# An expert stage on one core: adding products and transposes moved into the branches of the weight products

## The chip, the cores and the metric

The kernel runs on one core of a Trainium2 chip. The metric is the device time of one execution in microseconds (us), the median of several runs. The engines are TensorE (PE, matmuls; PEld is its weight load, PEq its sequencer), VectorE (DVE), ScalarE (ACT), GpSimd (POOL) and SyncE (SP, which issues the loads).

## The reference, cut to what matters

The program is two layers of a hybrid block on 256 tokens of 1024 channels, all in float32. The second layer ends in a mixture of eight experts; each token goes to the two experts with the highest router logits. This is the stage of the change:

```python
D_FF_EXPERT = 3584; N_EXPERTS = 8; TOP_K = 2
def swiglu(x, wg, wu, wd):
    return (jax.nn.silu(x @ wg) * (x @ wu)) @ wd
def moe_swiglu(x, router, wg, wu, wd):
    ...
    for e in range(N_EXPERTS):
        y = y + gate[:, e:e + 1] * swiglu(t, wg[e], wu[e], wd[e]).astype(jnp.float32)
```

## The kernel before, in words

**Tokens.** For each expert the kernel gathers that expert's tokens (at most 128, else a slow way at the end) into a tile `xg`, transposed, as two float32r parts that add up to the float32 value (a high and a low part). The same is done with every weight: a piece of 1 MB is loaded by SP into a tile `w` (or `big`), ACT rounds half a piece to its high part (line 347, 128x1024), and DVE subtracts to get the low part (line 348, 128x1024). Such a pair of halves is one tile `wp`; four of them rotate.

**Units.** The 3584 hidden columns of an expert are worked in seven slices of 512. A unit is one expert and one slice, 56 units in all. The loop in `moe` does for each unit, in this order: the gate half (`half_mm`, four weight products), the up half (`half_mm`, four), and then the down products of the unit before (`down`, four). One weight product (`products`) uses one pair of halves. So there are twelve pairs to a unit, and each needs one cast on ACT, one subtraction on DVE and one product on PE. The orders of PE, ACT and DVE in this stage are as the code writes them.

**Two branches.** PE reads how many tokens the expert has (`many[e]`). With more than 64 (`HALF`), a product is six matmuls (lines 376 to 378: high x high, high x low, low x high for two slices of the channels). With at most 64, the tokens' high and low part lie side by side in one stationary operand, and a product is four matmuls (line 1562). The rows 64 to 127 of the result then hold the low tokens' share, and it must be added to rows 0 to 63: ACT copies it to a tile `low` (line 1580, `lower`), and PE adds it with a matmul with a shifted identity, the adding product (`folded`, line 1586). In the branch of many tokens there is nothing to add; there `folded` multiplies zeros (line 1589), 64x8. `folded` has a branch of its own (line 1585).

**Transposes.** h = silu(gate) x up of a unit (`hidden`, line 1593, and `hidden_times`, line 1596; tile `sgm`) is transposed on PE in the next unit, between its gate and its up half (`turn`), with four 128x128 transposes (line 1603) or eight of 64 rows (line 1608), again in a branch of its own (line 1601). ACT and DVE then split the result into the two parts of `hT` (`split_from_psum`, lines 386 and 387), which the down products read.

The experts are worked in pairs; gathering the next pair's tokens, the way back (`scatter`) and the like are small tasks that stand between the halves (`little`).

Of the kernel before, what the change touches and what calls it, by code (L numbers as in the profile page):

```python
# [19 lines left out]
P = 128  # L20
S = 256
D = 1024
KT = D // P
# [43 lines left out]
HALF = CAP // 2  # L67
# [204 lines left out]
def tile_hybrid_block(  # L272
    ctx: ExitStack, tc: tile.TileContext,
    x, x_t, w_in, mla_w_uq, mla_w_ukv, small, vecs, w_out, ln1_w, ln1_b, ffn_wg, ffn_wu, ffn_wd,
    router, moe_wg, moe_wu, moe_wd, ln2_w, ln2_b, cst, out, stop=None, dbg=None,
):
    nc = tc.nc
    pe, act, dve, pool, sp = nc.tensor, nc.scalar, nc.vector, nc.gpsimd, nc.sync
# [4 lines left out]
    def gap(pl, n, tag):  # L283

        pl.tile([P, n // 4], F32, tag=tag, bufs=1, name=tag)
# [13 lines left out]
    def bank(name="pm"):  # L299
        return psm.tile([P, 512], F32, tag="bank", name=name)  # L300
# [5 lines left out]
    def kept(name):  # L306
        o, n = _OFF[name]
        return ck[:, o:o + n]

    ident = kept("ident")  # L310
# [63 lines left out]
    def mm3(ps, s, m, first, last):  # L374

        pe.matmul(ps, s[0], m[0], start=first, stop=False)  # L376
        pe.matmul(ps, s[0], m[1], start=False, stop=False)  # L377
        pe.matmul(ps, s[1], m[0], start=False, stop=last)  # L378
# [6 lines left out]
    def split_from_psum(hi, lo, ps):  # L385
        act.copy(hi, ps)  # L386
        dve.tensor_tensor(lo, ps, hi.bitcast(F32), op=OP.subtract)
# [1024 lines left out]
    def moe(mp, free_order):  # L1412
        nonlocal x_sb

        fold = mp.tile([P, HALF], F32R, tag="fold", name="fold")
# [16 lines left out]
        many = {}  # L1432
# [42 lines left out]
        def soon_one():  # L1475
            if waiting:
                waiting.pop(0)()

        def soon_all():
            while waiting:  # L1480
                waiting.pop(0)()
# [50 lines left out]
        hs = {}  # L1532
# [8 lines left out]
                except StopIteration:  # L1541
                    tasks.pop(0)

        def products(e, todo):

            def plain():
                for ps, st, m, first, last in todo:  # L1550
                    mm3(ps, (st[:, 0], st[:, 1]), m, first, last)

            if e not in many:
                plain()
                return
            with tc.If(many[e] > HALF) as cmp:
                plain()
            with cmp.Else():
                for part in range(2):
                    for ps, st, m, first, last in todo:  # L1560
                        both = st.rearrange("p a s -> p (a s)")[:, HALF:HALF + P]
                        pe.matmul(ps, both, m[part], start=first and part == 0,  # L1562
                                  stop=last and part == 1)

        def half_mm(e, after={}):
            xg = state[e][0]
            ps = bank()
            for k in range(0, KT, 2):
                if k % 4 == 0:
                    pcs = feed.next()  # L1570
                m = pcs[k % 4 // 2]
                products(e, [(ps, xg[:, k + i], [q[:, i] for q in m], k + i == 0, k + i == KT - 1) for i in range(2)])
                soon_one()
                after.get(k // 2, lambda: None)()
            return ps, [] if e in many else None

        def lower(ps, low):
            if low is not None:
                low.append(mp.tile([P, 512], F32R, tag="sgm", bufs=SGM, name="low"))
                act.copy(low[0][HALF:], ps[HALF:])  # L1580

        def folded(e, ps, low):
            if low is not None:
                low, = low
                with tc.If(many[e] <= HALF) as cmp:
                    pe.matmul(ps[:HALF], fold[HALF:], low[HALF:], start=False, stop=True, skip_group_check=True)
                with cmp.Else():

                    pe.matmul(ps[:HALF, :8], fold[:HALF], fold[:HALF, :8], start=False, stop=True, skip_group_check=True)

        def hidden(e, s, pg):
            hs[e, s] = mp.tile([P, 512], F32, tag="sgm", bufs=SGM, name="sgm")
            act.activation(hs[e, s], pg, AF.Silu)

        def hidden_times(e, s, pu):
            dve.tensor_tensor(hs[e, s], hs[e, s], pu, op=OP.mult)

        def turn(e, s):
            last = (e, s) == UNITS[-1]
            pt = bank()  # L1600
            with tc.If(many[e] > HALF) as cmp:
                for j in range(4):
                    pe.transpose(pt[:, j * P:(j + 1) * P], hs[e, s][:, j * P:(j + 1) * P], ident)
            with cmp.Else():
                for j in range(4):
                    for i in range(2):
                        c = j * P + i * HALF
                        pe.transpose(pt[:, c:c + HALF], hs[e, s][:HALF, j * P:(j + 1) * P], ident[:HALF, :HALF])
            if last:
                hT = mp.tile([P, 4, 2, P], F32R, tag=XG[5], name="hl")  # L1610
            else:
                if not gapped:
                    gap(mp, GAPS[1], "gap1")
                hT = mp.tile([P, 4, 2, P], F32R, tag="hT", bufs=HTB, name="hT")
                if not gapped:
                    gapped.append(gap(mp, GAPS[2], "gap2"))
            hs[e, s] = hT
            return lambda: split_from_psum(hT[:, :, 0], hT[:, :, 1], pt.rearrange("p (j s) -> p j s", j=4))

        def down(e, s, after={}):  # L1620
            if s == 0:
                z[e] = [bank("z") for _ in range(2)]
            hT = hs.pop((e, s))
            for j in range(2):
                pw = feed.next()
                last = (e, s, j) == (*UNITS[-1], 1)
                for i in range(2):
                    products(e, [(z[e][h], hT[:, 2 * j + k],
                                  [q[:, k] for q in pw[h]] if last else [q[:, 0, h * 512:(h + 1) * 512] for q in pw[k]],
                                  s == 0 and j == k == 0, s == NS - 1 and j == k == 1)  # L1630
                                 for k, h in ([(0, i), (1, i)] if last else [(i, 0), (i, 1)])])
                    soon_one()
                    after.get(2 * j + i, lambda: None)()

# [44 lines left out]
        first = gather(ORDER[0])  # L1679
# [5 lines left out]
        prev = None  # L1685
# [4 lines left out]
        for i_, (e, s) in [(i // (2 * NS), u) for i, u in enumerate(UNITS)]:  # L1690
            if s == 0:
                soon_all()
            end = (e, s) == UNITS[-1]
            pg, low_g = half_mm(e)
            little()
            split_hidden = turn(*prev) if prev else lambda: None
            pu, low_u = half_mm(e, {0: split_hidden, 1: lambda: lower(pg, low_g), 3: lambda: folded(e, pg, low_g)})
            little()
            if prev:
                def product():  # L1700
                    folded(e, pu, low_u)
                    hidden(e, s, pg)
                    if end:
                        hidden_times(e, s, pu)

                down(*prev, {0: lambda: lower(pu, low_u), 1 if end else 2: product,
                             3: (lambda: turn(e, s)()) if end else lambda: hidden_times(e, s, pu)})
                if prev[1] == NS - 1:
                    tasks.append(scatter(prev[0]))
                    if prev[0] == ORDER[i_ - 1][1]:  # L1710
                        tasks.append(way_back(ORDER[i_]))
                    little()
            else:
                lower(pu, low_u)
                folded(e, pu, low_u)
                hidden(e, s, pg)
                hidden_times(e, s, pu)
            if (e, s) == (0, 2):

                x_sb = xpool.tile([P, 2, D], F32, tag="x", name="x_sb")  # L1720
                for t in range(2):
                    pool.tensor_tensor(x_sb[:, t], xh[:, t].bitcast(F32), xl[:, t].bitcast(F32), op=OP.add)
                    pool.tensor_scalar(x_sb[:, t], x_sb[:, t], ALPHA, None, op0=OP.mult)
            if s == 3 and e == ORDER[i_][0] and i_ + 1 < len(ORDER):
                tasks.append(gather(ORDER[i_ + 1]))
            if s > 1:
                little()
            prev = (e, s)
# [16 lines left out]
        with tc.If(v > CAP):  # L1745
            for e in range(NE):
# [3 lines left out]
                xg = mp.tile([P, KT, P], F32, tag="xg0", name="xg2")  # L1750
                for k in range(KT):
                    ps = bank()
# [10 lines left out]
                with tc.For_i(0, D_FE, P) as f0:  # L1763
# [8 lines left out]
                    ps = bank()  # L1772
# [3 lines left out]
                    hT = mp.tile([P, 512], F32, tag="sgm", bufs=SGM, name="hT2")[:, :P]  # L1776
# [6 lines left out]
                pt = bank()  # L1783
# [8 lines left out]
                for h in range(2):  # L1792
                    dve.tensor_scalar(z2[h], z2[h], gsl, None, op0=OP.mult)
                    for t in range(2):
                        ps = bank()
# [10 lines left out]
        for t in range(2):  # L1806
# [6 lines left out]
            for h in range(2):  # L1813
                c = slice(h * 512, (h + 1) * 512)
# [79 lines left out]
```

## Time and profile before

| what | value |
|---|---|
| median of 3 runs | 1429.23 us (1426.94 to 1429.64) |
| profiled execution | 1427.92 us |
| its span | 1426.2 us |
| PE busy | 1378.8 us (97%) |
| DVE busy | 1240.4 us (87%) |
| ACT busy | 1048.9 us (74%) |
| read from HBM | 428.19 MB |

The span runs from the first to the last instruction of the profiled execution; the rest of its time lies around it. Busy times are of the whole program: the first layer and the mixer of the second come before the experts, whose first Silu starts at 473.8 us. Matmuls are pipelined, so a matmul's duration (0.39 us for 128x512) is longer than the step from one start to the next (0.23 us), and it is the steps that add up to time.

### The profile page before, as it was taken

The page shows a single profiled execution, that of the slowest core. Times are in us where ns is not written, and L with a number is a line of the kernel's source. Part 1 is how long each engine was busy: PE and PEld are TensorE (multiplying, and loading weights), DVE is VectorE, ACT ScalarE, POOL GpSimd, SP SyncE. Part 2 cuts the span into 40 slices and gives each one's busy share as a digit, 9 for nine tenths or more (in the row PEclk, how much of TensorE's full clock was granted, in tenths as well). Part 3 has the DMA queues.
Part 4 walks back from the last instruction along what each step waited for, and adds up shares of the span by engine and source line. Part 5 has one row for each costly group of instructions (what it writes and reads, how often), then busy time and mean ns, then how long its engine had stood idle before and what let it go on. Part 6 is the DMA issues. An engine that isn't in the chain of part 4 may idle for free. (4 is left out here: it accounts for less than half of the span.)

```text
span 1426.2 us, 20823 instructions
## 1 busy us (share of the span) xinstructions
PE 1378.8 (97%) x7068; PEld 1091.3 (77%) x7068; DVE 1240.4 (87%) x1702; ACT 1048.9 (74%) x1384; POOL 57.3 (4%) x70
## 2 busy tenths in 40 slices
PE   9999999999999989999999999999999999999995
PEld 8888999987888756666788766678887876667774
DVE  7998645468788999999988899998889899999896
ACT  7743534436633879899888889988888888998884
POOL 1020000001011040000000000000000000000000
PEclk9999999999999999999999999999999999999998
DMA  9364736562258979999999999999999999999950
GB/s 342 123 230 130 256 133 220 177 231 90 105 212 327 384 256 393 391 386 402 402 375 345 340 371 397 402 402 357 337 335 353 361 362 378 391 402 401 371 188 35
DMA packets 200045, 431.19 MB, mean 302 GB/s; under 512 B 9824, under 2 KB 44000, under 8 KB 199904
## 3 DMA queue, kind: packets, MB, share of 16 engines
q1 hardware_dynamic: 195952, 425.01, 81.4%
q0 software_dynamic: 864, 3.15, 0.6%
q8 instruction: 93, 1.52, 0.4%
q10 hardware_dynamic: 3088, 1.11, 0.4%
q14 instruction: 48, 0.39, 0.1%
HBM read 428.19 MB, written 1.05 MB: 301 GB/s over the span
## 5 line engine op out<-in xcount | busy, mean ns | idle before, releaser
L348 DVE TENSOR_TENSOR wp<-w,wp 128x1024 fp32r<-128x1024 f32 (+2 forms) x676 | 789.7, 1205 | 112.1 <-ACT wp L347 100.9
L347 ACT CAST wp<-w 128x1024 fp32r<-128x1024 f32 (+2 forms) x676 | 679.2, 1030 | 170.7 <-PE pm L383 38.2
L1562 PE MATMUL pm<-wp,xg 128*128 128x512 f32 x848 | 225.8, 411 | 19.0 <-DVE wp L348 17.7
L1562 PEld LDWEIGHTS pm<-wp,xg 128*128 128x128 f32 x848 | 153.6, 192 | 76.8 <-DVE wp L348 46.2
L377 PE MATMUL pm<-wp,xg 128*128 128x512 f32 x472 | 184.5, 391 | 2.9 <-DVE wp L348 2.9
L376 PE MATMUL pm<-wp,xg 128*128 128x512 f32 x472 | 186.8, 396 | 0.0
L378 PE MATMUL pm<-wp,xg 128*128 128x512 f32 x472 | 184.1, 390 | 0.0
L1562 PE MATMUL z<-wp,hT 128*128 128x512 f32 x448 | 129.3, 418 | 0.7 <-DVE wp L348 0.7
L348 DVE TENSOR_TENSOR wp<-big,wp 128x1024 fp32r<-128x1024 f32 x100 | 119.0, 1221 | 6.8 <-ACT wp L347 5.3
L347 ACT CAST wp<-big 128x1024 fp32r<-128x1024 f32 x100 | 102.3, 1051 | 11.7 <-PE pm L378 8.2
L1562 PEld LDWEIGHTS z<-wp,hT 128*128 128x128 f32 x448 | 75.6, 188 | 41.6 <-DVE wp L348 21.3
L377 PEld LDWEIGHTS pm<-wp,xg 128*128 128x128 f32 x472 | 88.7, 188 | 22.2 <-DVE wp L348 4.9
L378 PEld LDWEIGHTS pm<-wp,xg 128*128 128x128 f32 x472 | 88.6, 188 | 18.7
L376 PEld LDWEIGHTS pm<-wp,xg 128*128 128x128 f32 x472 | 88.7, 188 | 17.8
L381 PE MATMUL pm<-big,wp 128*128 128x256 f32 x320 | 90.6, 283 | 0.0
L383 PE MATMUL pm<-big,wp 128*128 128x256 f32 x320 | 90.6, 283 | 0.0
L382 PE MATMUL pm<-big,wp 128*128 128x256 f32 x320 | 90.5, 283 | 0.0
L376 PE MATMUL z<-wp,hT 128*128 128x512 f32 x216 | 89.1, 413 | 0.0
L377 PE MATMUL z<-wp,hT 128*128 128x512 f32 x216 | 84.9, 393 | 0.4 <-DVE wp L348 0.4
L378 PE MATMUL z<-wp,hT 128*128 128x512 f32 x216 | 84.0, 389 | 0.0
L520 PE MATMUL pm<-wp,big 128*128 128x512 f32 (+1 forms) x288 | 69.7, 389 | 0.6 <-ACT big L386 0.2
L1580 ACT CAST low<-pm 64x512 fp32r<-64x512 f32 x109 | 63.5, 583 | 2.6
(323 smaller groups left out, 1859.9 us busy)
## 6 DMA issues: line engine op xcount, KB each, us to landing
w<-in_moe_w_gate_dram SPq DMA_DIRECT2D x93, 1024.0 KB, 7.9
w<-in_moe_w_up_dram SPq DMA_DIRECT2D x93, 1024.0 KB, 7.7
w<-in_moe_w_down_dram SPq DMA_DIRECT2D x92, 1024.0 KB, 7.3
big<-in_moe_w_gate_dram SPq DMA_DIRECT2D x17, 1024.0 KB, 6.6
big<-in_moe_w_up_dram SPq DMA_DIRECT2D x17, 1024.0 KB, 6.7
w<-in_w_in_dram SPq DMA_DIRECT2D x16, 1024.0 KB, 8.5
big<-in_moe_w_down_dram SPq DMA_DIRECT2D x16, 1024.0 KB, 8.9
w<-in_ffn_w_gate_dram SPq DMA_DIRECT2D x11, 1024.0 KB, 5.6
```

Of the source, the lines that this page charges most:

```text
L347: act.copy(hv[c], src_[c])
L348: dve.tensor_tensor(lv[c], src_[c], hv[c].bitcast(F32), op=OP.subtract)
L376: pe.matmul(ps, s[0], m[0], start=first, stop=False)
L377: pe.matmul(ps, s[0], m[1], start=False, stop=False)
L378: pe.matmul(ps, s[1], m[0], start=False, stop=last)
L381: pe.matmul(ps, s[0], m[0], start=first, stop=False)
L382: pe.matmul(ps, s[1], m[0], start=False, stop=False)
L383: pe.matmul(ps, s[0], m[1], start=False, stop=last)
L520: pe.matmul(o, s, m, start=start, stop=stop)
L1562: pe.matmul(ps, both, m[part], start=first and part == 0, stop=last and part == 1)
L1580: act.copy(low[0][HALF:], ps[HALF:])
```

## The change

Three edits, all in what PE is given:

- `turn` can be joined: the transposes of a unit's h become the first instructions in both branches of the first product of the next unit's up half, in place of a branch of their own. This is done where both units belong to the same expert.
- The adding product becomes the last instruction in the short branch (few tokens) of a weight product: of the last product of the up half for the gate half, of the third down product for the up half (that one where both units belong to the same expert, and not in the last unit).
- The long branch (many tokens) gets nothing in its place. `folded` stays for the up half of each expert's first unit and of the last unit.

```diff
-        def products(e, todo):
+        def products(e, todo, first=((), ()), then_few=()):
...
             with tc.If(many[e] > HALF) as cmp:
+                for f in first[1]:
+                    f()
                 plain()
             with cmp.Else():
+                for f in first[0]:
+                    f()
                 for part in range(2):
...
-                        pe.matmul(ps, both, m[part], start=first and part == 0,
+                        pe.matmul(ps, both, m[part], start=begin and part == 0,
                                   stop=last and part == 1)
+                for f in then_few:
+                    f()
...
+        def fold_in(ps, low):
+            pe.matmul(ps[:HALF], fold[HALF:], low[0][HALF:], start=False, stop=True, skip_group_check=True)
...
-        def turn(e, s):
+        def turn(e, s, joined=False):
...
+            if not joined:
+                with tc.If(many[e] > HALF) as cmp:
+                    in_many()
+                with cmp.Else():
+                    in_few()
...
+            split = lambda: split_from_psum(hT[:, :, 0], hT[:, :, 1], pt.rearrange("p (j s) -> p j s", j=4))
+            return (split, ([in_few], [in_many])) if joined else split
...
-            split_hidden = turn(*prev) if prev else lambda: None
-            pu, low_u = half_mm(e, {0: split_hidden, 1: lambda: lower(pg, low_g), 3: lambda: folded(e, pg, low_g)})
+            split_hidden, first = lambda: None, ((), ())
+            if prev and prev[0] == e and e in many:
+                split_hidden, first = turn(*prev, True)
+            elif prev:
+                split_hidden = turn(*prev)
+            pu, low_u = half_mm(e, {0: split_hidden, 1: lambda: lower(pg, low_g)},
+                                first, {3: [lambda: fold_in(pg, low_g)]} if low_g is not None else {})
...
+                same = prev[0] == e and low_u is not None and not end
...
-                    folded(e, pu, low_u)
+                    if not same:
+                        folded(e, pu, low_u)
...
+                     {2: [lambda: fold_in(pu, low_u)]} if same else {})
```

On PE, at the start of the up half of a unit within an expert, this stood before (each branch's body follows its compare; the long branch is first; `pm` is a bank of PSUM, `ck` holds the identity, `sgm` is h):

```order
L1601 COMPARE_AND_BRANCH
L1603 MATMUL pm<-ck,sgm 128x128 x4
L1601 UNCONDITIONAL_BRANCH
L1608 MATMUL pm<-ck,sgm 128x64 x8
L1601 UNCONDITIONAL_BRANCH
L1556 COMPARE_AND_BRANCH
L376 MATMUL pm<-wp,xg 128x512
...
L1556 UNCONDITIONAL_BRANCH
L1562 MATMUL pm<-wp,xg 128x512 x4
L1556 UNCONDITIONAL_BRANCH
```

And this stands there now, on the same engine at the same place:

```order
L1557 COMPARE_AND_BRANCH
L1615 MATMUL pm<-ck,sgm 128x128 x4
L376 MATMUL pm<-wp,xg 128x512
...
L1557 UNCONDITIONAL_BRANCH
L1621 MATMUL pm<-ck,sgm 128x64 x8
L1567 MATMUL pm<-wp,xg 128x512 x4
L1557 UNCONDITIONAL_BRANCH
```

The transposes have moved past one compare and one jump into the product's two bodies; their number, shape and place among the matmuls are the same.

On PE, at the end of the up half (line 1586 adds, line 1589 multiplies zeros; `z` is the sum of the down products), this stood before:

```order
L1562 MATMUL pm<-wp,xg 128x512 x4
L1556 UNCONDITIONAL_BRANCH
L1585 COMPARE_AND_BRANCH
L1586 MATMUL pm<-low,fold 64x512
L1585 UNCONDITIONAL_BRANCH
L1589 MATMUL pm<-fold 64x8
L1585 UNCONDITIONAL_BRANCH
L1556 COMPARE_AND_BRANCH
L376 MATMUL z<-wp,hT 128x512
```

And this stands there now:

```order
L1567 MATMUL pm<-wp,xg 128x512 x4
L1591 MATMUL pm<-low,fold 64x512
L1557 UNCONDITIONAL_BRANCH
L1557 COMPARE_AND_BRANCH
L376 MATMUL z<-wp,hT 128x512
```

The adding product has moved up into the short branch behind its four matmuls, and the product of zeros is gone, so that the long branch goes from its last matmul to the next product. The other engines' instructions stand in the same order as before, apart from their jumps from block to block.

## Rows read from the trace of the kernel before

**Rows 1.** The page: busy time of each engine (share), instructions.

```profile
PE 1378.8 (97%) x7068; PEld 1091.3 (77%) x7068; DVE 1240.4 (87%) x1702; ACT 1048.9 (74%) x1384; POOL 57.3 (4%) x70
```

**Rows 2.** Busy time by stretch (start:end, length, engines, granted clock, DMA share, GB/s).

```profile
634.66:649.49 14.83, 14.29 (x59) 9.07 (x59) 14.83 (x15) 14.03 (x16) 0.00 (x0) 1.00 1.04 406
807.86:822.62 14.76, 14.55 (x63) 10.86 (x62) 14.61 (x15) 14.03 (x16) 0.00 (x0) 1.00 1.02 373
914.90:931.48 16.58, 16.58 (x77) 12.79 (x77) 15.75 (x15) 14.53 (x17) 0.00 (x0) 1.00 1.04 409
931.48:950.75 19.27, 18.29 (x82) 14.43 (x80) 18.99 (x21) 15.59 (x19) 0.00 (x0) 1.00 1.04 398
1097.92:1115.46 17.54, 17.54 (x80) 14.01 (x78) 15.65 (x14) 14.75 (x16) 0.00 (x0) 1.00 1.00 359
511.25:518.10 6.85, 5.64 (x13) 4.05 (x14) 6.85 (x6) 3.57 (x5) 6.76 (x3) 0.50 0.71 245
```

**Rows 3.** Waits, 634.66 to 664.30 (two short units): us in total, times, longest.

```profile
PE pm L1562 <- DVE wp L348: 1.1, 2, 0.5
```

**Rows 4.** Waits, 1097.92 to 1150.54 (three long units).

```profile
ACT wp L347 <- PE pm L378: 5.5, 18, 0.3
DVE wp L348 <- ACT wp L347: 3.9, 9, 0.5
```

**Rows 5.** Groups of PE by line: busy us, mean ns, idle before.

```profile
L1586 PE MATMUL pm<-low,fold 64*64 64x512 f32 x53 | 23.3, 439 | 0.0
L1589 PE MATMUL pm<-fold 64*64 64x8 f32 x56 | 12.2, 217 | 0.0
```

**Rows 6.** Timeline of PE at a product of zeros, long unit: start, length.

```profile
1110.19 0.39 PE L378 MATMUL pm<-wp,xg 128*128 128x512 f32 x1
...
1110.87 0.39 PE L378 MATMUL pm<-wp,xg 128*128 128x512 f32 x1
1111.19 0.22 PE L1589 MATMUL pm<-fold 64*64 64x8 f32 x1
1111.34 0.50 PE L376 MATMUL z<-wp,hT 128*128 128x512 f32 x1
1111.67 0.40 PE L377 MATMUL z<-wp,hT 128*128 128x512 f32 x1
1111.91 0.39 PE L378 MATMUL z<-wp,hT 128*128 128x512 f32 x1
```

**Rows 7.** Timeline of PE at the transposes of a long unit.

```profile
1104.94 0.39 PE L378 MATMUL pm<-wp,xg 128*128 128x512 f32 x1
1105.17 0.60 PE L1603 MATMUL pm<-ck,sgm 128*128 128x128 f32 x4
1105.52 0.48 PE L376 MATMUL pm<-wp,xg 128*128 128x512 f32 x1
1105.84 0.40 PE L377 MATMUL pm<-wp,xg 128*128 128x512 f32 x1
```

**Rows 8.** Branch records of PE's sequencer, two lines: duration ns min/median/max.

```profile
L1585 PEldq COMPARE_BRANCH  x162: 67/176/298, 485.8 to 1395.0; - x162
L1601 PEldq COMPARE_BRANCH  x84: 65/176/334, 478.3 to 1399.6; - x84
```

**Rows 9.** Timeline of ACT at the copy of hT, two long units.

```profile
940.18 0.59 ACT L386 CAST hT<-pm 128x512 fp32r<-128x512 f32 x1 [0.29 <-PE pm L1603]
941.58 1.05 ACT L347 CAST wp<-w 128x1024 fp32r<-128x1024 f32 x1 [0.81 <-PE pm L378]
...
1106.32 0.58 ACT L386 CAST hT<-pm 128x512 fp32r<-128x512 f32 x1
```

**Rows 10.** Timeline of PE at two waits for DVE.

```profile
509.15 0.73 PE L1562 MATMUL pm<-wp,xg 128*128 128x512 f32 x2 [2.14 <-DVE wp L348]
...
937.37 0.50 PE L377 MATMUL pm<-wp,xg 128*128 128x512 f32 x1 [0.98 <-DVE wp L348]
```

More of the change, by code (lines that the diff above doesn't have):

```diff
@@ L1542, in little @@
                     tasks.pop(0)
-        def products(e, todo):
+        def products(e, todo, first=((), ()), then_few=()):
             def plain():
-                for ps, st, m, first, last in todo:
-                    mm3(ps, (st[:, 0], st[:, 1]), m, first, last)
+                for ps, st, m, begin, last in todo:
+                    mm3(ps, (st[:, 0], st[:, 1]), m, begin, last)
             if e not in many:
@@ L1556, in products, with half_mm @@
             with tc.If(many[e] > HALF) as cmp:
+                for f in first[1]:
+                    f()
                 plain()
             with cmp.Else():
+                for f in first[0]:
+                    f()
                 for part in range(2):
-                    for ps, st, m, first, last in todo:
+                    for ps, st, m, begin, last in todo:
                         both = st.rearrange("p a s -> p (a s)")[:, HALF:HALF + P]
-                        pe.matmul(ps, both, m[part], start=first and part == 0,
+                        pe.matmul(ps, both, m[part], start=begin and part == 0,
                                   stop=last and part == 1)
-        def half_mm(e, after={}):
+                for f in then_few:
+                    f()
+        def half_mm(e, after={}, first=((), ()), few={}):
             xg = state[e][0]
@@ L1571, in half_mm @@
                 m = pcs[k % 4 // 2]
-                products(e, [(ps, xg[:, k + i], [q[:, i] for q in m], k + i == 0, k + i == KT - 1) for i in range(2)])
+                products(e, [(ps, xg[:, k + i], [q[:, i] for q in m], k + i == 0, k + i == KT - 1) for i in range(2)],
+                         first if k == 0 else ((), ()), few.get(k // 2, ()))
                 soon_one()
@@ L1580, in lower @@
                 act.copy(low[0][HALF:], ps[HALF:])
+        def fold_in(ps, low):
+            pe.matmul(ps[:HALF], fold[HALF:], low[0][HALF:], start=False, stop=True, skip_group_check=True)
         def folded(e, ps, low):
             if low is not None:
-                low, = low
                 with tc.If(many[e] <= HALF) as cmp:
-                    pe.matmul(ps[:HALF], fold[HALF:], low[HALF:], start=False, stop=True, skip_group_check=True)
+                    fold_in(ps, low)
                 with cmp.Else():
@@ L1596, in hidden_times, with in_many, in_few @@
             dve.tensor_tensor(hs[e, s], hs[e, s], pu, op=OP.mult)
-        def turn(e, s):
+        def turn(e, s, joined=False):
             last = (e, s) == UNITS[-1]
             pt = bank()
-            with tc.If(many[e] > HALF) as cmp:
+            h_ = hs[e, s]
+            def in_many():
                 for j in range(4):
-                    pe.transpose(pt[:, j * P:(j + 1) * P], hs[e, s][:, j * P:(j + 1) * P], ident)
-            with cmp.Else():
+                    pe.transpose(pt[:, j * P:(j + 1) * P], h_[:, j * P:(j + 1) * P], ident)
+            def in_few():
                 for j in range(4):
@@ L1607, in turn @@
                         c = j * P + i * HALF
-                        pe.transpose(pt[:, c:c + HALF], hs[e, s][:HALF, j * P:(j + 1) * P], ident[:HALF, :HALF])
+                        pe.transpose(pt[:, c:c + HALF], h_[:HALF, j * P:(j + 1) * P], ident[:HALF, :HALF])
+            if not joined:
[3 more added lines that the diff above has]
+                    in_few()
             if last:
@@ L1617, in turn, with down @@
             hs[e, s] = hT
-            return lambda: split_from_psum(hT[:, :, 0], hT[:, :, 1], pt.rearrange("p (j s) -> p j s", j=4))
-        def down(e, s, after={}):
+            split = lambda: split_from_psum(hT[:, :, 0], hT[:, :, 1], pt.rearrange("p (j s) -> p j s", j=4))
+            return (split, ([in_few], [in_many])) if joined else split
+        def down(e, s, after={}, few={}):
             if s == 0:
@@ L1630, in down @@
                                   s == 0 and j == k == 0, s == NS - 1 and j == k == 1)
-                                 for k, h in ([(0, i), (1, i)] if last else [(i, 0), (i, 1)])])
+                                 for k, h in ([(0, i), (1, i)] if last else [(i, 0), (i, 1)])], then_few=few.get(2 * j + i, ()))
                     soon_one()
@@ L1706, in moe @@
                 down(*prev, {0: lambda: lower(pu, low_u), 1 if end else 2: product,
-                             3: (lambda: turn(e, s)()) if end else lambda: hidden_times(e, s, pu)})
+                             3: (lambda: turn(e, s)()) if end else lambda: hidden_times(e, s, pu)},
+                     {2: [lambda: fold_in(pu, low_u)]} if same else {})
                 if prev[1] == NS - 1:
```

## The prediction

> **What bounds the kernel now.** I read the page first: TensorE (PE) is busy for 97% of the span, VectorE (DVE) for 87%, ScalarE (ACT) for 74% [rows 1]. Such shares are means over stages, so I cut the expert stage (from about 473 us to the end) into its units by the Silu of each unit on ACT, and asked for the busy times of single units. Two kinds appear [rows 2].
>
> In a unit of an expert with few tokens (short branch) DVE is busy 14.83 us of 14.83 us, and PE 14.29. The units of this kind without extra work all take 14.81 to 14.83 us. In two such units PE's matmuls idle for DVE's lower half once each, for 0.5 us [rows 3]. So here DVE sets the pace and PE has slack.
>
> In a unit of an expert with many tokens (long branch) PE is busy 17.54 us of 17.54 us and DVE only 15.65. The waits run the other way: ACT waits for PE's matmuls to free a pair of halves, DVE waits for ACT [rows 4]. Here PE sets the pace. The lines of transposes and products place the experts: 2, 4, 5 and 7 take the long branch, 0, 1, 3 and 6 the short one, 28 units each. A change on PE is worth something in the first four alone.
>
> **The products of zeros.** They ran 56 times, all in long branches [rows 5]. What one costs is more than its own 0.22 us or 0.15 us of issue. Start to start in [rows 6]: from the L378 at 1110.87 past the zero product to the L378 at 1111.91 is 1.04 us for three steps of 128x512 matmuls; the three steps just before it, from 1110.19 to 1110.87, took 0.68. The difference is 0.36 us: the zero product starts 0.09 late behind a full matmul, and the second matmul after it 0.10 late, so the change of tile size (64x64, then 128x128 again) is paid on both sides. A check by the unit: 72 matmuls x 0.227 = 16.34; two zero products 0.72; the four transposes 0.45 (from 1104.94 to 1105.84 is 0.90 for two steps that otherwise take 0.45 [rows 7]); sum 17.51, measured 17.54.
>
> How many go: each unit has one for the gate half and one for the up half. The up-half one stays where the previous unit is another expert's (first unit of experts 2, 4, 5, 7) and in the very last unit: 5 stay, 51 go. 51 x 0.36 = 18.4 us, if each is paid on a path that PE sets.
>
> Is it? A steady long unit becomes 17.54 - 0.72 = 16.82 us. DVE's 15.65 still fits, with 1.17 us left. The weights of a unit are 12 halves x 128 x 1024 x 4 bytes = 6.29 MB; in 16.82 us that asks 374 GB/s, and a short unit shows 406 [rows 2], so the loads keep up. Where an expert with many tokens starts, one unit holds a wait for DVE (0.98 us at 937.37 [rows 10]; experts 2, 4 and 7), but DVE idles 0.28 us within that unit and 0.83 us in the one before it [rows 2], so PE being earlier lets DVE start earlier. Where experts 2 and 5 hand over to a short one, DVE is busy 14.61 of 14.76 us [rows 2]: the last product of zeros ahead of it can pass on only about 0.15 of its 0.36. I take off 0.2 twice: 18.4 - 0.4 = 18.0 us.
>
> **The adding products, joined.** In the short branch the adding product runs as before, once for each half, behind the same matmuls and with the same wait for ACT's copy; only its branch goes (101 of 109 places in the program). The branch records on PE's sequencer last 176 ns in the median, 67 at the least, 298 at the most [rows 8]. Cover in the short branch: DVE, which has no idle time there. Cover in the long branch: the branch of the transposes stands between the L378 at 1104.94 and the first transpose at 1105.17, and their step is 0.23 us [rows 7] as between matmuls of one product (0.68 for three [rows 6]); the sequencer is ahead of the array. So I cost the branches at nothing. If the cover were gone in the long units, each turn and each adding product would give back a branch and a jump, at most 0.176 + 0.067 = 0.24 us: (24 turns + 51) x 0.24 = 18 us more. Below nothing: a joined body is longer to jump over; the longest record of the turn's branch is 334 ns against 176 [rows 8], so at most 0.16 x 48 joined turns = 8 us, in PE time that in the short half of them is hidden. I take zero, by the rows on gaps.
>
> The Trainium skill ("Advanced Engine Details and Errata", Control Flow Timing) gives about 108 ns for a compare-and-branch and 51 ns for a plain one; the records here are longer, so the measurement decides. By the page's figures as an exposed cost the estimate would be 75 x 0.16 = 12 us more of gain; by the gaps it is none.
>
> **The transposes of h, joined.** Same number, shape and place in PE's order, and every other engine's real work keeps its order. One thing moves: ACT's copy of hT. In the built program its semaphore count is reached by the eighth transpose in the short branch, as before, but in the long branch by the second matmul behind the four transposes. By [rows 7] that is 1105.84 + 0.40 = 1106.24 instead of 1105.77, 0.47 us later. In a steady long unit ACT starts this copy at 1106.32 anyway, since it is busy with a cast until then [rows 9]. In the second unit of an expert ACT already idled 0.29 us for the transposes (at 940.18 [rows 9]); there it comes up to 0.47 us later, but ACT then idles 0.81 us for PE anyway (next row). Cost 0. Bounds: 0, and 24 x 0.47 = 11 us given back if each delay reached PE.
>
> **Sum.** Against the profiled execution, 1427.92 us (span 1426.2): 1427.92 - 18.0 = 1409.9. The median of the runs is 1.3 us above the profiled one, so the forecast is 1411 us. Its own range is 1408 to 1414: gains of 15 to 21 us against the median.
>
> **Rivals.**
> 1. The price of a zero product is only its slot. If the late second matmul (1111.34 to 1111.67) waited for its own operand and not for the change of tile size, it would stay, 0.36 falls to about 0.24 (0.32 + 0.15 - 0.23) and the gain to 51 x 0.24 = 12 us: 1417. For it: it is an L377, the one that reads DVE's half. Against it: three such units list no wait of PE for DVE [rows 4], and the second matmul behind the transposes is as late (0.32 [rows 7]).
> 2. The branches cost too, at the upper bound above: another 18 us, 1393. For it: records of 176 ns. Against it: no gap at them.
> 3. The copy of hT takes the place: ACT's delay passes to DVE and PE, 11 us back, 1422. Against it: ACT idles 2.8 us in a steady long unit (14.75 of 17.54 [rows 2]).
> 4. All is hidden, because another engine or the loads fill the time: 1429. Against it: DVE's 1.9 us idle in each long unit.
> 5. Slower: the clock. PE's granted clock was 0.50 (1.2 GHz) from 511.25 to 518.10 [rows 2], after a wait of 2.14 us for DVE that ended at 509.15 [rows 10]. After 0.98 us at 937.37 it stayed at 1.00 (2.4 GHz) [rows 2, 10]. The place is the short units: there the change can only lengthen PE's wait for DVE, once per unit (0.5 us of idle now [rows 3]). If the three branches gone per unit were all paid today (3 x 0.24 = 0.7) that wait would be 1.2 us; it decides when that wait is like the one before the fall, about 2.1. The price: 6.85 us at half clock hold 3.4 us of work; the wait covers 2.1 of the loss, so 1.3 us are lost in each of 24 units, 31 us, against 18 gained: 1442. Against it: 1.2 is below 2.1, and PE gains next to nothing in these units. The Trainium skill ("TensorE: Matmul & The Clock Gate", Why this matters for your kernels) has the same rule in general: idle gaps between bursts of matmuls bring the lower clock back; the fall at 511 agrees.
>
> **How the numbers follow.** Forecast 70%, rival 1 10%, rival 2 5%, rival 3 6%, rival 4 5%, rival 5 4%. A measurement of this kernel tells 0.2% (2.9 us) from no change. Faster: forecast and rivals 1 to 3, 0.91. Same: rival 4, 0.05. Slower: rival 5, 0.04. The range takes in rival 1 and some extra gain from branches: 1405 to 1420.
>
> **What would show it.** Right: steady long units of 16.8 us with DVE idle near 1.2; short units unchanged at 14.8; 5 products of zeros left, at 0.36 each; 0.23 us from the last up-half matmul to the first down-half one. Wrong: a step of 0.33 us still there at the start of the down half (rival 1); ACT idle before hT growing together with PE's waits for DVE in long units (3); granted clock of 0.50 at new places (5); long units under 16.6 us (2).

## The result and the profile after

The changed kernel takes 1411.51 us (median of 4 runs, 1409.78 to 1411.83) against 1428.74 us before (4 runs in the same session): ratio 0.9879, 95% interval 0.9864 to 0.9895, so 17.2 us less (15.0 to 19.4 by the interval). The profiled execution took 1411.74 us with a span of 1410.0.

The page's first line answers to [rows 1]: PE is 18 us less busy, 51 matmuls fewer, and still at 97%.

```profile
PE 1360.8 (97%) x7017; PEld 1086.4 (77%) x7017; DVE 1235.0 (88%) x1702; ACT 1049.0 (74%) x1384; POOL 57.3 (4%) x70
```

The same stretches as in [rows 2], each from one unit's Silu to the next one's (start:end, length, PE, PEld, DVE, ACT, POOL, granted clock, DMA share, GB/s): a steady short unit; the handover from expert 2 to 3; into expert 4; its first unit to its second; a steady long unit.

```profile
635.11:649.92 14.81, 14.28 (x59) 9.07 (x59) 14.81 (x15) 14.01 (x17) 0.00 (x0) 1.00 1.04 406
804.42:819.17 14.75, 14.54 (x62) 10.40 (x60) 14.60 (x15) 14.05 (x16) 0.00 (x0) 1.00 1.02 365
911.45:928.07 16.62, 16.62 (x77) 13.07 (x77) 15.74 (x15) 14.54 (x17) 0.00 (x0) 1.00 1.04 408
928.07:946.95 18.88, 17.71 (x80) 14.12 (x79) 18.73 (x21) 15.58 (x18) 0.00 (x0) 1.00 1.04 398
1088.75:1105.57 16.82, 16.82 (x78) 13.91 (x77) 15.46 (x15) 14.75 (x17) 0.00 (x0) 1.00 1.02 378
```

The steady long unit went from 17.54 to 16.82 us, PE still without a gap; the short unit did not move and DVE is still its bound. The loads gave the 378 GB/s that the faster unit asks for.

PE's timeline where a product of zeros stood [rows 6]: the last matmul of the up half, then the first three of the down half.

```profile
1101.34 0.39 PE L378 MATMUL pm<-wp,xg 128*128 128x512 f32 x1
1101.57 0.39 PE L376 MATMUL z<-wp,hT 128*128 128x512 f32 x1
1101.79 0.39 PE L377 MATMUL z<-wp,hT 128*128 128x512 f32 x1
1102.02 0.39 PE L378 MATMUL z<-wp,hT 128*128 128x512 f32 x1
```

Three steps take 0.68 us; with the product of zeros they took 1.04. What is left of those products and of the branches of the adding products (answers by line; min/median/max ns):

```profile
L1599 PE MATMUL pm<-fold x5: 217/217/217, 695.1 to 1382.0; 64*64 64x8 f32 x5
```

```profile
L1595 PEldq COMPARE_BRANCH  x11: 67/176/219, 585.6 to 1379.3; - x11
```

ACT's timeline at the copy of hT, second unit of expert 4 and a steady long unit [rows 9]:

```profile
937.24 0.59 ACT L386 CAST hT<-pm 128x512 fp32r<-128x512 f32 x1 [0.75 <-PE pm L377]
...
1096.79 0.58 ACT L386 CAST hT<-pm 128x512 fp32r<-128x512 f32 x1
```

In the second unit ACT now idles 0.75 us and names L377, the second matmul, where it idled 0.29 us for the transposes; in the steady unit it does not idle. And PE's one wait for DVE in expert 4 [rows 10]:

```profile
933.96 0.50 PE L377 MATMUL pm<-wp,xg 128*128 128x512 f32 x1 [1.17 <-DVE wp L348]
```

It grew from 0.98 to 1.17 us.

For what follows the profiles are also compared by one stretch, here called the long stretch: from the Silu of expert 2's first unit to the last Silu of the stage. It holds the long units, all but the start of expert 2's first and the end of the last, and the short units of experts 3 and 6. It took 702.33 us before and 686.16 after, 16.2 us less, and repeats to about 0.1 us between kernels that should agree in it.

### The profile page after: what moved, and what is told of

The parts are those of the page before. It is cut to its first block, busy times and chain, and to the rows that moved or that the text cites. A ratio compares the mean times of both kernels' runs of the same rounds, so it can differ in the third digit from the quotient of the medians.

```text
span 1410.0 us, 20525 instructions
## 1 busy us (share of the span) xinstructions
PE 1360.8 (97%) x7017; PEld 1086.4 (77%) x7017; DVE 1235.0 (88%) x1702; ACT 1049.0 (74%) x1384; POOL 57.3 (4%) x70
## 5 line engine op out<-in xcount | busy, mean ns | idle before, releaser
L377 PE MATMUL pm<-wp,xg 128*128 128x512 f32 x472 | 184.9, 392 | 3.5 <-DVE wp L348 3.5
L376 PE MATMUL pm<-wp,xg 128*128 128x512 f32 x472 | 186.8, 396 | 0.0
L378 PE MATMUL pm<-wp,xg 128*128 128x512 f32 x472 | 184.2, 390 | 0.0
L1567 PE MATMUL z<-wp,hT 128*128 128x512 f32 x448 | 129.1, 417 | 1.1 <-DVE wp L348 1.1
L377 PEld LDWEIGHTS pm<-wp,xg 128*128 128x128 f32 x472 | 88.8, 188 | 23.7 <-DVE wp L348 6.4
L378 PEld LDWEIGHTS pm<-wp,xg 128*128 128x128 f32 x472 | 88.6, 188 | 18.5
L376 PEld LDWEIGHTS pm<-wp,xg 128*128 128x128 f32 x472 | 88.7, 188 | 17.8
L376 PE MATMUL z<-wp,hT 128*128 128x512 f32 x216 | 85.0, 393 | 0.0
L377 PE MATMUL z<-wp,hT 128*128 128x512 f32 x216 | 84.4, 391 | 0.4 <-DVE wp L348 0.4
L378 PE MATMUL z<-wp,hT 128*128 128x512 f32 x216 | 84.1, 389 | 0.0
```

What stands on the lines that cost most here:

```text
L1567: pe.matmul(ps, both, m[part], start=begin and part == 0, stop=last and part == 1)
```

## The experiments

**One part of the change at a time.** First the kernel before without the products of zeros, and nothing else changed:

```diff
                 with tc.If(many[e] <= HALF):
                     pe.matmul(ps[:HALF], fold[HALF:], low[HALF:], ...)
-                with cmp.Else():
-                    pe.matmul(ps[:HALF, :8], fold[:HALF], fold[:HALF, :8], ...)
```

Expected: 

> The kernel before with the products of zeros alone removed (all 56; every branch stays, the adding products and transposes stay in branches of their own). Theory (the gain of 17 us is the products of zeros, 0.36 us each in long units; branches cost nothing): 1411 us, ratio 0.988, steady long units 16.8 us. Rival (branches are part of the gain): 1417 to 1425, steady long units 17.0 to 17.4 us. If branches were dear (0.24 us for each of 75 in long units), this kernel would lie 18 us above the changed one.

Measured: 1439.56 us, ratio 1.0075 (1.006 to 1.009). It is slower than before, which neither the theory nor the rival expected. A steady long unit and, inside it, PE's timeline at one of the now empty branches, and the sequencer's records on that line:

```profile
1105.21:1123.19 17.98, 17.35 (x78) 13.75 (x76) 15.74 (x14) 14.75 (x16) 0.00 (x0) 1.00 0.99 351
```

```profile
1105.06 0.39 PE L378 MATMUL z<-wp,hT 128*128 128x512 f32 x1
1105.77 0.49 PE L376 MATMUL z<-wp,hT 128*128 128x512 f32 x1 [0.32 <-PEq L1585]
1106.09 0.39 PE L377 MATMUL z<-wp,hT 128*128 128x512 f32 x1
1106.32 0.39 PE L378 MATMUL z<-wp,hT 128*128 128x512 f32 x1
```

```profile
L1585 PEldq EVENT_SEMAPHORE  x56: 51/51/51, 693.4 to 1409.7; - x56
```

PE's matmuls count up a semaphore that the other engines wait for, and the count must be the same whichever branch was taken. In the built program the empty branch gets an instruction of the sequencer that waits until PE's own count has reached that of its earlier matmuls, and then adds the one that the adding product would have added. There were none on this line before; now there are 56. Three steps take 1.26 us, 0.58 more than without anything and 0.22 more than with a product of zeros: 56 x 0.22 = 12 us, and 10.4 were measured. So the product of zeros was the cheaper way to keep the count. In the changed kernel the join put the adding product into a branch whose other side has matmuls of its own to count with, and the product of zeros could go without such a wait: the steps there are 0.23 us (above).

Then the other way round, the joins with the products of zeros put back behind the last matmul of the long branch:

```diff
                 plain()
+                for f in then_many:     # the product of zeros, 64x8
+                    f()
```

Expected: 

> The changed kernel with the products of zeros put back, as the last instruction in the long branch of the weight product (51 places on the long path), so both joins stay. Theory: the whole gain is gone, 1428 to 1429 us, ratio 1.00, steady long units 17.5 us. Rival (the joins give part): 1415 to 1424.

Measured: 1428.71 us, ratio 0.9997 (0.9987 to 1.0006); the long stretch 702.41 us. The gain is gone to the last tenth.

```profile
1099.83:1117.38 17.55, 17.55 (x80) 14.01 (x78) 15.65 (x14) 14.76 (x17) 0.00 (x0) 1.00 1.00 361
```

The transposes alone, joined in the kernel before, and apart again in the changed one (the edit is that of the second; the first is the changed kernel with `folded` back in all its places and no `fold_in`):

```diff
-            if prev and prev[0] == e and e in many:
+            if False:
                 split_hidden, first = turn(*prev, True)
```

Expected of the first: 

> The kernel before with only the transposes joined; adding products and products of zeros stay in their own branches. Theory: no change, ratio 1.000 within 0.2%, steady long units 17.5 us, short 14.8 us. Rival (a branch costs 0.24 us in each of 24 long units): 6 us less, ratio 0.996. Rival (the later copy of hT costs): up to 11 us more, ratio 1.008.

Expected of the second: 

> The changed kernel with the transposes in a branch of their own again; adding products joined, products of zeros gone. Theory: as the changed kernel, 1411 us, ratio to before 0.988. Rival (a branch costs 0.24 us): 1417, ratio 0.992. If the later copy of hT cost anything in the changed kernel, this one would be faster than it, down to 1400, and ACT's copy of hT would start 0.47 us earlier behind the transposes where ACT idles.

Measured: 1428.98 us, ratio 1.000 (0.9991 to 1.0009), long stretch 702.35; and 1411.11 us, ratio 0.9876 (0.9861 to 0.9891), long stretch 686.18. A steady long unit of the second:

```profile
1088.25:1105.06 16.81, 16.81 (x78) 13.90 (x77) 15.46 (x15) 14.74 (x17) 0.00 (x0) 1.00 1.01 377
```

and ACT at the copy of hT in its second unit of expert 4:

```profile
936.19 0.59 ACT L386 CAST hT<-pm 128x512 fp32r<-128x512 f32 x1 [0.29 <-PE pm L1615]
937.59 1.05 ACT L347 CAST wp<-w 128x1024 fp32r<-128x1024 f32 x1 [0.81 <-PE pm L378]
```

Joining the transposes neither gains nor costs. The copy does start 0.46 us earlier where ACT idles for it, and that reaches nobody.

**What the 0.36 us are.** Three kernels put another product of zeros into the same 51 places of the changed kernel (the lines are cut to the product itself):

```diff
-  pe.matmul(ps[:HALF, :8], fold[:HALF], fold[:HALF, :8], ...)                    # as it was, 64x64 tile
+  pe.matmul(ps[:, :8], none[:, :1].to_broadcast([P, P]), fold[:, :8], ...)       # 128x128 tile, 8 columns
+  for _ in range(2): pe.matmul(ps[:HALF, :8], fold[:HALF], fold[:HALF, :8], ...) # two of them
+  pe.matmul(ps[:HALF], none[:HALF, :1].to_broadcast([HALF, HALF]), xg0..., ...)  # 64x64 tile, 512 columns
```

Expected of the 128x128 tile: 

> The changed kernel with a product of zeros put back in the 51 places at the end of the long branch, but with the 128x128 tile of its neighbours (a stationary operand of zeros, 8 columns moving) in place of 64x64. Theory (the 0.36 us is the change of tile size, paid on both sides): a step of at most 0.11 us as the transposes have, 51 x 0.11 = 6 us, 1417 us. Rival (a short matmul does not cover the next weight load, whatever its tile): 0.2 to 0.3 us each, 1422 to 1427.

Expected of two: 

> The changed kernel with two 64x64 products of zeros, one behind the other, in each of the 51 places. Theory (change of tile size): the second one costs its own slot alone, 0.06 to 0.15 us: 1428.7 + 3 to 8 = 1432 to 1437, ratio 1.002 to 1.006. Rival (each instruction has the full price): 1428.7 + 18 = 1447, ratio 1.013.

Expected of 512 columns: 

> The changed kernel with a 64x64 product of zeros of 512 columns in place of 8 in each of the 51 places. Theory (change of tile size, both sides): 0.36 + 0.21 for the columns = 0.57 us, 51 x 0.57 = 29 us, 1440, and the second matmul behind it still 0.1 us late. Rival (the late second matmul is an uncovered weight load): 512 columns cover it, 0.3 to 0.45 us each, 1427 to 1434, second matmul at 0.23.

Measured: 1417.53 us (ratio 0.9926, 0.9909 to 0.9942); 1431.59 us (1.0024, 1.0014 to 1.0035); 1438.95 us (1.0071, 1.0054 to 1.0088). PE's timelines, the 128x128 tile first, then two, then 512 columns:

```profile
1104.99 0.39 PE L378 MATMUL pm<-wp,xg 128*128 128x512 f32 x1
1105.22 0.17 PE L1597 MATMUL pm<-fold,none 128*128 128x8 f32 x1
1105.25 0.48 PE L376 MATMUL z<-wp,hT 128*128 128x512 f32 x1
1105.56 0.40 PE L377 MATMUL z<-wp,hT 128*128 128x512 f32 x1
1105.80 0.39 PE L378 MATMUL z<-wp,hT 128*128 128x512 f32 x1
```

```profile
1113.16 0.39 PE L378 MATMUL pm<-wp,xg 128*128 128x512 f32 x1
1113.47 0.28 PE L1597 MATMUL pm<-fold 64*64 64x8 f32 x2
1113.68 0.50 PE L376 MATMUL z<-wp,hT 128*128 128x512 f32 x1
1114.02 0.39 PE L377 MATMUL z<-wp,hT 128*128 128x512 f32 x1
1114.25 0.40 PE L378 MATMUL z<-wp,hT 128*128 128x512 f32 x1
```

```profile
1105.03 0.39 PE L378 MATMUL z<-wp,hT 128*128 128x512 f32 x1
1105.35 0.45 PE L1597 MATMUL pm<-xg,none 64*64 64x512 f32 x1
1105.72 0.50 PE L376 MATMUL z<-wp,hT 128*128 128x512 f32 x1
1106.06 0.39 PE L377 MATMUL z<-wp,hT 128*128 128x512 f32 x1
1106.29 0.39 PE L378 MATMUL z<-wp,hT 128*128 128x512 f32 x1
```

Over the 0.68 us of three plain steps these are 0.13, 0.41 and 0.58 us. With the tile of its neighbours the extra product starts on time (0.23 behind L378) and lets the next one start at once (0.03). At 8 columns the change of tile size and back thus makes 0.23 of the 0.36 us, and it is paid once for two products in a row (the second adds 0.05). At 512 columns it makes more: one more 128x512 matmul in the long branch costs 0.24 us (measured further below), the 64x64 one 0.58, which leaves 0.34.

The second matmul behind the product is late in all three timelines: 0.31, 0.34 and 0.34 us instead of 0.23. So neither the shortness of the product nor the change of tile alone explains it. It is late behind 8 columns without a change of size, and behind 512 columns with one; the rival of the third run, that 512 columns would bring it back to 0.23, falls. The weight loads show what the cases share. PEld's timelines: the kernel before, then the 128x128 tile, then 512 columns:

```profile
1111.19 0.13 PEld L1589 LDWEIGHTS pm<-fold 64*64 64x64 f32 x1 [0.35 <-ACT wp L347]
1111.34 0.19 PEld L376 LDWEIGHTS z<-wp,hT 128*128 128x128 f32 x1
1111.44 0.19 PEld L377 LDWEIGHTS z<-wp,hT 128*128 128x128 f32 x1
```

```profile
1105.00 0.19 PEld L1597 LDWEIGHTS pm<-fold,none 128*128 128x128 f32 x1
1105.22 0.19 PEld L376 LDWEIGHTS z<-wp,hT 128*128 128x128 f32 x1
1105.33 0.19 PEld L377 LDWEIGHTS z<-wp,hT 128*128 128x128 f32 x1
```

```profile
1105.35 0.13 PEld L1597 LDWEIGHTS pm<-xg,none 64*64 64x64 f32 x1 [0.35 <-ACT wp L347]
1105.72 0.19 PEld L376 LDWEIGHTS z<-wp,hT 128*128 128x128 f32 x1 [0.25 <-issue]
1105.83 0.19 PEld L377 LDWEIGHTS z<-wp,hT 128*128 128x128 f32 x1
```

In the changed kernel, with nothing between, L376's weights begin to load at 1101.34 for a matmul at 1101.57, together with the matmul before it. The 128x128 product keeps to that: its load begins at 1105.00 and the next at 1105.22, each together with the matmul before. Around a 64x64 product, of 8 or of 512 columns, the product's load and the next one begin only with their own matmuls (1111.19 and 1111.34; 1105.35 and 1105.72): nothing is loaded ahead across the change of tile. In the built program all three products wait for ACT's count alone, and the 128x128 one starts on time, so it is not ACT, which the bracket names, that holds the others. And in all three cases L377 starts 0.33 or 0.34 us after L376's load began: the late second matmul goes with a load that began at most 0.03 us ahead of its own matmul, where a plain stream has 0.23. With the 64x64 tile that is so at 8 and at 512 columns; with the 128x128 tile it comes about because L376 starts 0.03 us behind the short product. Why a change of tile holds the loads back, no run here shows.

With the 128x128 product of 8 columns in the kernel before, in the adding products' own branches, no branch moved:

Expected: 

> The kernel before, every branch as it was, but the 56 products of zeros have the 128x128 tile of their neighbours (stationary zeros, 8 columns). Theory (a branch costs nothing; a product of zeros that fits the tile costs 0.13 us, and the kernel without any lost its gain to the wait that stands in the empty branch): 1411.5 + 56 x 0.13 = 1418 to 1419, ratio 0.993. Rival (an adding product in a branch of its own costs 0.2 us or more whatever stands in it): 1428 to 1435.

Measured: 1417.04 us, ratio 0.9924 (0.9907 to 0.994), long stretch 691.55 against 691.60 with the joins. Two thirds of the change's gain come without any join, and a branch of its own costs the adding product nothing as long as something in it counts.

```profile
1091.39:1108.45 17.06, 17.06 (x80) 14.12 (x79) 15.48 (x15) 14.75 (x16) 0.00 (x0) 1.00 1.01 366
```

**What covers PE in the short units.** The changed kernel with 56 more matmuls of 128x512 (stationary zeros), once in the short branches and once in the long ones:

```diff
+                if more:    # second product of each gate and up half
+                    pe.matmul(todo[0][0], none[:, :1].to_broadcast([P, P]), todo[0][2][0], start=False, stop=False)
```

Expected in the short branch: 

> The changed kernel with one more 128x512 matmul (a stationary operand of zeros, real weights moving, so the sums stay) in the second product of each half, gate and up, in the short branch: 56 matmuls, 0.23 us each, 12.7 us of PE time. Theory (DVE sets the pace of the short units): no change, 1411 to 1413, short units still 14.8 us. Rival (PE's time counts there): 1424, short units 15.3 us.

Expected in the long branch: 

> Control to the kernel with one more matmul in the short branch: the same 128x512 matmul in the second product of each half, gate and up, but in the long branch, 56 matmuls. Theory (PE sets the pace of the long units): 56 x 0.227 = 12.7 us more than the changed kernel, 1424, steady long units 17.25 us. Rival (the 1.3 us that DVE idles in a long unit takes it up): 1411 to 1414.

Measured: 1412.31 us, ratio 0.9887 (0.987 to 0.9903); and 1425.53 us, ratio 0.9977 (0.9968 to 0.9987). A short unit of the first and a long unit of the second:

```profile
635.81:650.64 14.83, 14.29 (x61) 9.54 (x61) 14.83 (x15) 14.01 (x16) 0.00 (x0) 1.00 1.04 405
```

```profile
1096.32:1113.62 17.30, 17.30 (x80) 14.28 (x79) 15.62 (x15) 14.75 (x16) 0.00 (x0) 1.00 1.02 367
```

The same work is free where DVE is busy all the time, and costs 0.24 us apiece where PE is. (PE's busy time in the short unit is 14.29 us with the two matmuls and 14.28 without: a matmul's record of 0.39 us covers more than its step, so busy time hides slack of this size.)

**Where an expert with many tokens starts.** The changed kernel with the product of zeros put back for the gate half of first units alone:

Expected: 

> The changed kernel with the 64x64 product of zeros put back for the gate half of each expert's first unit only (four on the long path, experts 2, 4, 5, 7). Theory (in experts 2, 4 and 7 its going was worth nothing, since PE then waits for DVE that much longer in the next unit; only expert 5's was worth 0.36 us): 1411 to 1413, the wait in the second unit 1.0 us of idle as before instead of 1.17. Rival (it was worth 0.36 us each, 1.4 in all): the stretch from that unit to the next is 0.36 us longer in each.

Measured: 1412.8 us in one run, too little to tell by; the profile tells. PE's wait in expert 4's second unit is back at its old length (0.97 us; in experts 2 and 7 it is 0.97 and 0.98, against 1.17 and 1.18 in the changed kernel), the stretch from Silu to Silu there is 18.90 us as without it (18.88), and only the stretch into expert 5 is longer, 17.01 us against 16.65 in the changed kernel:

```profile
934.74 0.50 PE L377 MATMUL pm<-wp,xg 128*128 128x512 f32 x1 [0.97 <-DVE wp L348]
```

```profile
1037.11:1054.12 17.01, 17.01 (x78) 13.70 (x76) 15.64 (x15) 14.72 (x17) 0.00 (x0) 1.00 1.00 357
```

No version came out that beats the changed kernel by more than a measurement tells: its last five products of zeros could be given the 128x128 tile, 5 x 0.23 = 1.2 us at most, part of it behind the waits just shown. That was not run.

## Why the prediction was right

- **What bounds which unit**: right, and shown by the pair of added matmuls.
- **The price of a product of zeros**: right in size. The unit was forecast at 16.82 us and takes 16.82; DVE's idle time 1.17, measured 1.36. The reason given, "the change of tile size is paid on both sides", holds as far as it goes: around 64x64 products of 8 and of 512 columns no weights are loaded ahead on either side. It is not the whole price: a product of 8 columns with the tile of its neighbours costs 0.13 us too, with the second matmul nearly as late (0.31 us against 0.33), so only 0.23 of the 0.36 us would go with the tile alone.
- **51 of 56 go**: right, 5 are left.
- **"PE being earlier lets DVE start earlier"**: wrong. Ahead of the wait in experts 2, 4 and 7, DVE's idle time hardly shrank (in expert 4 from 0.83 to 0.88 us in one unit and from 0.28 to 0.15 in the next), the wait grew by 0.19 to 0.20 us, and two steps of PE at the start of the second unit of expert 4 took 0.14 longer (from 928.15 to 928.75 in the changed kernel, 0.60 for 0.46). The three products there were worth nothing: 1.1 us less gain, shown by putting them back.
- **The handover to a short expert**: too kind. The stretch is 14.75 us after, 14.76 before; the last product's 0.36 us is lost whole, not 0.2 of it: 0.3 us over the two.
- **Branches at nothing**: right for the turns (two kernels) and for the adding products (the 128x128 product in own branches). Rival 2 falls. What the forecast did not see is why the join was needed: a branch with nothing in it is dear.
- **The copy of hT**: right, 0.46 us later where ACT idles, no cost. Rival 3 falls.
- **Rival 1** (0.24 us a product) falls with the unit's 16.82 us and the step of 0.22 us where its 0.33 would have stayed; **rival 4** with the result; **rival 5** too: the clock is at 1.00 in the short units of which rows are shown, before and after.
- **The sum**: 18.0 us were forecast, and the long stretch gave 16.17. Another 0.46 us shows only behind the last Silu (28.12 us from there to the end of the span before, 27.66 after): the last step from Silu to Silu holds two products and gained only 0.37 us (16.21 to 15.84). That makes 16.6 us, and the two misses above make the remaining 1.4.
- **The median**: that it fell by 17.2 us and hit the forecast within 0.5 us is in part luck, as the products' share is 16.6. The two profiled executions differ by 16.2 us, and two places that have nothing to do with the change lie in that. About 1.1 us lie in experts 0 and 1 (221.93 and 220.86 us from the first Silu to expert 2's): in the profile of before the granted clock fell a second time, and in that of after it did not. And 1.5 us the other way lie ahead of the first Silu (at 473.77 and 475.29 us): there the granted clock of after was 0.51 from 458.55 to 461.95 us, and that of before 1.00. The kernel with the products of zeros put back has its first Silu at 475.71 us too.

Of before, then of after, the stretch in question (granted clock third from the end):

```profile
593.17:600.00 6.83, 6.83 (x22) 5.31 (x22) 6.64 (x8) 3.67 (x6) 0.00 (x0) 0.50 1.05 402
```

```profile
593.00:601.00 8.00, 7.74 (x35) 5.46 (x36) 8.00 (x10) 6.27 (x8) 0.00 (x0) 1.00 1.04 401
```

The changed kernel with the transposes apart has this second fall too and takes 222.0 us there, so it is not the change that sets it. Nor does the length of PE's wait ahead of it, by which rival 5 was judged, tell the two apart: it was 1.84 us before (ended at 591.75) and 1.86 after (593.25), both below the 2.1 that the forecast took as its mark.

The same 32 matmuls ahead of the first Silu, before, then after, at the two levels of the clock:

```profile
457.32 4.37 PE L1497 MATMUL pm<-oh,big 128*128 128x256 f32 x32 [1.07 <-DVE oh L1487]
457.36 5.85 PE L1497 MATMUL pm<-oh,big 128*128 128x256 f32 x32 [1.07 <-DVE oh L1487]
```

## What to carry to other kernels

Price an instruction by the steps of its neighbours with and without it, not by its own duration: a product of 8 columns, 0.22 us by its own record, cost 0.36. A time saved ahead of a wait for another engine is not passed on unless that engine was itself waiting for the saved work, so count the places one by one. And an empty branch is not free: see what keeps the semaphore's count in it before an instruction that does nothing is taken out.

## What the runs showed of the hardware that was not expected

- A 64x64 matmul between 128x128 ones costs 0.23 us more than one of 8 columns with their tile, and 0.34 us more than one of 512 columns with their tile; two of 8 columns in a row pay it once. Its weights, and those of the matmul behind it, began to load only with their own matmuls, where in a plain stream a load begins one matmul ahead.
- A matmul of 8 columns with the tile of its neighbours costs 0.13 us; the second matmul behind it starts 0.08 us late, as it does behind the transposes (0.32 against 0.23). In each of these cases it started 0.33 or 0.34 us after the load for the matmul ahead of it had begun.
- A wait of PE's sequencer for PE's own matmuls costs 0.58 us over three steps in a dense stream, more than a useless matmul with a change of tile (0.36).
